# Value products of two attention heads issued in turn, one in each half of TensorE's columns

## The chip, the cores and the metric

One core of a Trainium2 chip runs the whole program. The metric is device time in microseconds of one execution; lower is better. The engines that matter here are TensorE (PE, with its weight loads listed as PEld), VectorE (DVE), ScalarE (ACT) and GpSimd (POOL).

## The reference

Two transformer-like blocks at 512 tokens and width 1024. What touches the change is its attention, always with heads of 64 values:

```python
# block 1: eight heads of dilated causal attention (beside a gated delta rule)
# block 2, even layer: eight neighbourhood heads, each of 512 queries over
#   a window of 256 keys and 256 context keys; eight heads of context over context;
#   and four differential heads of 128 values:
p1 = softmax(q1 @ k1.T * scale)
p2 = softmax(q2 @ k2.T * scale)
y  = (p1 - lam * p2) @ v
# block 2, odd layer: eight query heads over two key/value heads, 768 keys
p  = softmax(qg @ k.T * d ** -0.5)
y  = p @ v                      # the value product
```

## The kernel before

All attention works on tiles of 128 queries by 128 keys, in float32. For one head and one query tile there are four steps. *score*: TensorE writes the scores to PSUM, VectorE takes the row maximum, ScalarE the exponential into a tile E (helper `exp_rows`). *turn*: TensorE transposes E, 128 columns at a time, and ScalarE or VectorE copies the result into a tile PT (`pt_tiles`). *apply*: TensorE multiplies values and PT, one matmul for each key tile, summed in a PSUM bank `pv`. *end*: the bank is scaled by the row sums, which TensorE spreads over partitions with eight small matmuls on a tile `rr` (`bcast`, line 431), again 64 columns at a time.

Heads come in pairs. Head 0 of a pair has its result in partitions 0 to 63 of the bank, head 1 in 64 to 127. A value tile is 128 rows by 64 columns, so one product uses 64 of the array's 128 columns: head 0 the first half, head 1 the second. Before the change each head has an apply of its own, which runs through all its key tiles:

```python
for kt in range(qt + 1):
    c = (2 * pair + e) * 64
    PE.matmul(st["v", pair][hs, qs], self.dv[:, kt, c:c + 64], pt[:, kt * P:(kt + 1) * P],
              start=kt == 0, stop=kt == qt)
```

There are three such places: `dilated` (block 1, line 955, key tiles 1 to 4 by the query tile), `neighbourhood` (line 1664, 4 key tiles) and `pair_attention` (line 1723, the context heads of the even layer with 2 key tiles and the odd layer with 6). Differential attention (`diff_attention`, line 1779) uses all 128 columns and keeps its own apply; each of its query tiles makes two E tiles, e1 and e2, which VectorE (line 1764) and GpSimd (lines 1768 and 1769) merge into e1 before the transposes.

`skewing` sets the program order: in each round it calls, for items that follow one another, the later steps first. On top of it a scheduler with a timeline of its own orders the instructions of each engine when the program is built. At run time every engine takes its instructions in that order and waits on semaphores.

E, PT and q tiles come from rings of a fixed number of buffers; the writer of a new tile waits until the last reader of the tile that had that buffer is done. Before, E has 5 buffers in the even and odd layers, PT has 2.

Of the kernel before, what the change touches and what calls it, by code (L numbers as in the profile page):

```python
# [10 lines left out]
F32 = mybir.dt.float32  # L11
# [7 lines left out]
P = 128  # L19
D = 1024  # L20
KD = 8
T = 512
C = 256
TC = T + C
# [198 lines left out]
class Prog:  # L223
# [686 lines left out]
    def dilated(self, da, ps, om):  # L910
        V, S, G, PE, Q, A = self.V, self.S, self.G, self.PE, self.Q, self.A
        psa = lambda: self.bank(ps, "a")
        kzs = self.zeroed(da, T)
        st = {}
        items = []
        for pair in range(4):
            for qt in range(4):
                for e in range(2):
                    n = (qt + 1) * P
                    qs = slice(qt * P, (qt + 1) * P)  # L920
                    hs = slice(64 * e, 64 * e + 64)

                    def load(pair=pair, qt=qt, e=e, qs=qs):
                        if qt == 0:
                            strip = st["b", e] = da.tile([P, T], F32, name="strip", bufs=2)
                            Q.dma_start(strip, self.dstrip[2 * pair + e])
                            if e == 0:
                                room = self.wr.tile([P, CH], F32, name="wraw").bitcast(F32R)
                                st["k", pair] = self.stacked(da, self.dk[:, pair], "k", kz=kzs[pair % 2],
                                                             st=[room[:, :T], room[:, T:]])  # L930
                        if e == 0:
                            st["q", pair, qt] = self.doubled(da, self.dq[:, pair, qs], "q", 3)

                    def score(pair=pair, qt=qt, e=e, n=n, qs=qs, hs=hs):
                        if qt == 0 and e == 0:
                            st["r", pair] = da.tile([P, 4, 2], F32, name="rr", bufs=2)
                        p = psa()
                        (q, lo), (k, kz) = st["q", pair, qt], st["k", pair]
                        self.scores(p[:, :n], (q[:, e], lo), (k[e][:, :n], kz[e][:, :n]))
                        st["e", pair, qt, e] = self.exp_rows(da, p[:, :n], n, st["b", e][:, T - n:],  # L940
                                                             r=st["r", pair][:, qt, e:e + 1])[0]

                    def turn(pair=pair, qt=qt, e=e, n=n):
                        p = psa()
                        self.transpose4(p, st["e", pair, qt, e], qt + 1)
                        pt = st["t", pair, qt, e] = da.tile([P, T], F32, name="PT", tag="PT", bufs=2)
                        S.activation(pt[:, :n], p[:, :n], AF.Copy)

                    def apply(pair=pair, qt=qt, e=e, qs=qs, hs=hs):
                        if qt == 0 and e == 0:  # L950
# [12 lines left out]
        return items  # L963

    def finish_pair(self, pool, prb, pv, rr, dst, nt=4):

        n = nt * P
        for t in range(nt):
            for e in range(2):
                self.bcast(prb[64 * e:64 * e + 64, t * P:(t + 1) * P], rr[:, t, e:e + 1], 64)  # L970
        rs = pool.tile([P, T], F32, name="rs", tag="PT", bufs=2)
        self.S.activation(rs[:, :n], prb[:, :n], AF.Copy)
# [612 lines left out]
    def scores(self, p, q, k):  # L1585
# [22 lines left out]
    def neighbourhood(self, consts, values, at, ps, qa, ka, vc, vad, oms):  # L1608
# [5 lines left out]
        st = {}  # L1614
        items = []
        count = 0
        for pair in range(4):
            for b in range(4):
                x = (0, 1, 1, 2)[b]
                for e in range(2):  # L1620
# [22 lines left out]
                    def score(pair=pair, b=b, e=e, bt=bt):  # L1643
# [8 lines left out]
                        self.scores(p[:, 256:512], q, [a[:, T:TC] for a in k])  # L1652
                        st["e", pair, b, e] = self.exp_rows(at, p[:, 0:T], T, bt, TC, st["r", pair][:, b, e:e + 1], 5)[0]
# [4 lines left out]
                    def apply(pair=pair, b=b, e=e):  # L1658
                        if b == 0 and e == 0:
                            st["v", pair] = self.bank(ps, "pv")  # L1660
                        c = slice((2 * pair + e) * 64, (2 * pair + e) * 64 + 64)
                        for kt in range(4):
                            lhs = st["vw", b // 2][:, b % 2, kt, c] if kt < 2 else vc[:, kt - 2, c]
                            PE.matmul(st["v", pair][64 * e:64 * e + 64, b * P:(b + 1) * P], lhs,
                                      st["t", pair, b, e][:, kt * P:(kt + 1) * P], start=kt == 0, stop=kt == 3)

# [23 lines left out]
    def pair_attention(self, at, ps, qT, form, keys, nk, nq, vals, dst):  # L1690
# [6 lines left out]
        for t in range(nq):  # L1697
            for e in range(2):
                hs = slice(64 * e, 64 * e + 64)

                def load(t=t):
# [5 lines left out]
                def score(t=t, e=e):  # L1707
# [5 lines left out]
                    self.scores(p, q, st["k", e])  # L1713
                    st["e", t, e] = self.exp_rows(at, p[:, 0:n], n, None, TC, st["r"][:, t, e:e + 1], 5)[0]

                def turn(t=t, e=e):
                    st["t", t, e] = self.pt_tiles(at, ps, st["e", t, e], nk)

                def apply(t=t, e=e, hs=hs):
                    if t == 0 and e == 0:  # L1720
                        st["v"] = self.bank(ps, "pv")
                    for kt in range(nk):
                        PE.matmul(st["v"][hs, t * P:(t + 1) * P], vals(e, kt), st["t", t, e][:, kt * P:(kt + 1) * P],  # L1723
                                  start=kt == 0, stop=kt == nk - 1)
# [5 lines left out]
                items.append([load if e == 0 else None, None, score, turn, apply,  # L1730
                              end if t == nq - 1 and e == 1 else None])
        return items

    def diff_attention(self, at, ps, qkb, vb, lam, oms, kzs):
# [5 lines left out]
        for hd in range(4):  # L1740
            for t in range(6):
# [9 lines left out]
                def score(hd=hd, t=t, k0=k0, n=n):  # L1751
# [326 lines left out]
```

## Time and profile before

| what | value |
|---|---|
| median of 3 runs | 2650.19 us (2647.8 to 2650.38) |
| profiled execution, its own time | 2653.09 us |
| span of that execution, first to last instruction | 2651.1 us |
| TensorE busy | 94% of the span |
| VectorE, GpSimd, ScalarE busy | 62%, 45%, 38% |
| mean granted clock of TensorE | 0.973 of 2.4 GHz |

The profiled execution is 2.9 us above the median; 2.0 us of its time lie outside the span. The attention of the program lies in four stretches of the span: dilated (228 to 366 us), differential (1131 to 1250), neighbourhood and context (1250 to 1337), and the odd layer's (2084 to 2187.5).

### The profile page before, as it was taken

To read this page: it belongs to the slowest core of one execution; us is meant where nothing else is said; L and a number is where in the kernel's file an instruction comes from. 1 tells how busy PE (TensorE), PEld (TensorE's weight loads), DVE (VectorE), ACT (ScalarE), POOL (GpSimd) and SP (SyncE) were. 2 spreads that over 40 slices of the span, in tenths; PEclk is the share of its full clock that TensorE was granted. 3 is DMA by queue.
4 is the path that set the end of the run, shared out by engine and by line. 5 is a ranking of instruction groups with operands and counts; after the bars stand their busy time and mean duration, and the time that the engine had idled before them with its cause. 6 is when DMAs were issued, how large, how long until landed. Compare 5 with 4: busy or idle time off the path is not lost.

```text
span 2651.1 us, 35356 instructions
## 1 busy us (share of the span) xinstructions
PE 2500.5 (94%) x13312; PEld 2078.7 (78%) x13312; DVE 1631.5 (62%) x2896; ACT 996.5 (38%) x1763; POOL 1192.6 (45%) x835
## 2 busy tenths in 40 slices
PE   7878999999999987977999999999999999999999
PEld 5657876788888766766888888888888888788887
DVE  6987556635334798778747677767577446634333
ACT  4424534322224423377634222121244553323232
POOL 3346535555555443577623233323245326444443
PEclk9999999999999998988999999999999999999999
DMA  5252022232333344301132343424242104232333
GB/s 196 77 183 62 25 63 96 87 96 86 103 99 96 128 143 131 131 17 29 45 119 88 106 137 114 140 96 152 72 128 80 32 26 142 88 96 88 103 96 95
DMA packets 103453, 257.94 MB, mean 97 GB/s; under 512 B 11745, under 2 KB 20065, under 8 KB 102900
## 3 DMA queue, kind: packets, MB, share of 16 engines
q1 hardware_dynamic: 102708, 254.64, 29.8%
q8 instruction: 105, 1.72, 0.3%
q10 hardware_dynamic: 576, 1.05, 0.1%
q14 instruction: 64, 0.52, 0.1%
HBM read 246.06 MB, written 14.83 MB: 98 GB/s over the span
## 4 chain that ended last, share of the span: by engine, by line
PE 73%; DVE 17%; DMA 3%; issue 2%; POOL 2%; ACT 2%; SPq 0%; POOLq 0%; DVEq 0%; ACTq 0%
PE ps_mm L323 14%; PE ps_mm L325 14%; PE ps_mm L324 14%; PE ps_mx L324 3%; PE ps_mx L325 3%; PE ps_mx L323 3%; PE ps_m L324 3%; PE ps_m L323 3%; PE ps_m L325 3%; PE ps_t L435 2%; DVE ada_w L1094 2%; DVE ada_j L1094 2%; PE ps_s L1593 2%; PE ps_pv L1723 2%; DMA ada_w<-in_w_ada 2%
## 5 line engine op out<-in xcount | busy, mean ns | idle before, releaser
L312 POOL TENSOR_TENSOR wlo<-wraw,whi 128x1024 fp32r<-128x1024 f32 (+2 forms) x344 | 777.0, 2262 | 1102.1 <-ACT whi L311 1016.7
L311 ACT ACTIVATE whi<-wraw 128x1024 fp32r<-128x1024 f32 (+2 forms) x345 | 336.7, 978 | 955.0 <-PE ps_mm L324 473.2
L323 PE MATMUL ps_mm<-h,whi 128*128 128x512 f32 (+1 forms) x1496 | 540.5, 363 | 11.7 <-ACT whi L311 7.2
L325 PE MATMUL ps_mm<-h,wlo 128*128 128x512 f32 (+1 forms) x1496 | 539.3, 361 | 2.6 <-POOL wlo L312 2.5
L324 PE MATMUL ps_mm<-h,whi 128*128 128x512 f32 (+1 forms) x1496 | 539.5, 361 | 1.1 <-DVE h L1146 1.0
L323 PEld LDWEIGHTS ps_mm<-h,whi 128*128 128x128 f32 x1496 | 282.1, 189 | 56.8 <-ACT whi L311 7.2
L325 PEld LDWEIGHTS ps_mm<-h,wlo 128*128 128x128 f32 x1496 | 281.9, 189 | 49.1 <-POOL wlo L312 3.2
L324 PEld LDWEIGHTS ps_mm<-h,whi 128*128 128x128 f32 x1496 | 282.1, 189 | 47.6 <-issue 1.7
L1094 DVE CUSTOM_DVE_ANT_0 ada_j<-ada_w,ada_c 128x512 f32<-128x512 f32 x192 | 184.3, 960 | 13.1 <-DMA ada_w<-in_w_ada 12.6
L325 PE MATMUL ps_mm<-fa,wlo 128*128 128x512 f32 (+1 forms) x528 | 186.2, 356 | 1.7 <-POOL wlo L312 1.7
L1094 DVE CUSTOM_DVE_ANT_0 ada_w<-ada_w,ada_c 128x512 f32<-128x512 f32 x192 | 185.2, 965 | 4.0
L324 PE MATMUL ps_mm<-fa,whi 128*128 128x512 f32 (+1 forms) x528 | 187.6, 356 | 0.0
L323 PE MATMUL ps_mm<-fa,whi 128*128 128x512 f32 (+1 forms) x528 | 185.8, 356 | 0.0
L1271 DVE SCALAR_TENSOR_TENSOR cb<-ps_mm,small,cb 128x511 f32<-128x511 f32 (+1 forms) x66 | 43.6, 660 | 188.8 <-ACT cb L1269 188.8
L1219 DVE SCALAR_TENSOR_TENSOR x<-ps_mm,mod,x 128x512 f32<-128x512 f32 x80 | 59.5, 748 | 138.5 <-PE ps_mm L325 131.7
L325 PEld LDWEIGHTS ps_mm<-fa,wlo 128*128 128x128 f32 x528 | 99.0, 188 | 18.2 <-POOL wlo L312 2.3
L323 PEld LDWEIGHTS ps_mm<-fa,whi 128*128 128x128 f32 x528 | 98.9, 188 | 16.6 <-ACT whi L311 0.5
L324 PEld LDWEIGHTS ps_mm<-fa,whi 128*128 128x128 f32 x528 | 99.2, 188 | 16.0
L435 PE MATMUL ps_t<-ident,E 128*128 128x128 f32 x464 | 79.9, 292 | 20.4 <-POOL E L1769 13.6
L903 DVE TENSOR_REDUCE nm<-ps_s 128x1 f32<-128x768 f32 (+1 forms) x96 | 73.7, 774 | 38.7 <-PE ps_s L1593 37.8
L324 PE MATMUL ps_mx<-h,whi 128*128 128x512 f32 x216 | 86.2, 399 | 3.0 <-DVE h L1006 3.0
L323 PE MATMUL ps_mx<-h,whi 128*128 128x512 f32 x216 | 85.7, 398 | 0.5 <-ACT whi L311 0.5
(500 smaller groups left out, 5239.1 us busy)
## 6 DMA issues: line engine op xcount, KB each, us to landing
ada_w<-in_w_ada SPq DMA_DIRECT2D x192, 256.0 KB
wraw<-in_w_up SPq DMA_DIRECT2D x88, 512.0 KB
wraw<-in_w_d SPq DMA_DIRECT2D x48, 384.0 KB
wraw<-in_w_d SPq DMA_DIRECT2D x53, 320.0 KB
wraw<-in_we_in SPq DMA_DIRECT2D x24, 512.0 KB
wraw<-in_w_g SPq DMA_DIRECT2D x22, 512.0 KB
wraw<-in_w_u SPq DMA_DIRECT2D x22, 512.0 KB
wraw<-in_we_out SPq DMA_DIRECT2D x13, 512.0 KB
```

The source lines that it names most:

```text
L311: self.S.activation(hi[:, :n], raw[:, :n], AF.Copy)
L312: (eng or self.G).tensor_tensor(out=lo[:, :n], in0=raw[:, :n], in1=hi.bitcast(F32)[:, :n], op=ALU.subtract)
L323: mm(ps, lhi, rhi, start=start, stop=False)
L324: mm(ps, lhi, rlo, start=False, stop=False)
L325: mm(ps, llo, rhi, start=False, stop=stop)
L435: last = self.PE.transpose(ps[:, j * P:(j + 1) * P], src[:, j * P:(j + 1) * P], self.ident)
L903: V.tensor_reduce(out=m, in_=src, op=ALU.max, axis=AX.X, negate=True)
L1094: V.tensor_tensor_reduce(out=(junk, w)[s], in0=w, in1=c[:, s, i * T:i * T + T], scale=0.5, scalar=0.0, op0=ALU.mult, op1=ALU.add, accum_ou ...
L1219: V.scalar_tensor_tensor(out=xs[s][:, m], in0=p[:, :w], scalar=mod[:, gate * 8 + m, s:s + 1], in1=xs[s][:, m], op0=ALU.mult, op1=ALU.add)
L1271: V.scalar_tensor_tensor(out=cb[:, t0 + 1:t1], in0=pg[s][:, :w_ - 1], scalar=fw[0], in1=cb[:, t0 + 1:t1], op0=ALU.mult, op1=ALU.add)
L1593: self.PE.matmul(p[:, c0:min(n, c0 + 512)], q[i], k[i][:, c], start=i == 0, stop=i == 1)
L1723: PE.matmul(st["v"][hs, t * P:(t + 1) * P], vals(e, kt), st["t", t, e][:, kt * P:(kt + 1) * P], start=kt == 0, stop=kt == nk - 1)
```

## The change

A new helper issues the products of both heads of a pair in one step, key tile by key tile, head 0 and head 1 in turn. It runs in the item of head 1, when both PT tiles exist. To hold two PT tiles longer, PT goes from 2 to 3 buffers everywhere; E goes from 5 to 4 in the even and odd layers, and q from 3 to 2 in the dilated one.

```diff
@@ dilated
-                            st["q", pair, qt] = self.doubled(da, self.dq[:, pair, qs], "q", 3)
+                            st["q", pair, qt] = self.doubled(da, self.dq[:, pair, qs], "q", 2)
...
-                        pt = st["t", pair, qt, e] = da.tile([P, T], F32, name="PT", tag="PT", bufs=2)
+                        pt = st["t", pair, qt, e] = da.tile([P, T], F32, name="PT", tag="PT", bufs=3)
...
-                        pt = st["t", pair, qt, e]
-                        for kt in range(qt + 1):
-                            c = (2 * pair + e) * 64
-                            PE.matmul(st["v", pair][hs, qs], self.dv[:, kt, c:c + 64], pt[:, kt * P:(kt + 1) * P],
-                                      start=kt == 0, stop=kt == qt)
+                        self.apply_pair(st["v", pair], qs, qt + 1,
+                                        lambda e, kt: self.dv[:, kt, (2 * pair + e) * 64:(2 * pair + e) * 64 + 64],
+                                        [st["t", pair, qt, e] for e in range(2)])
...
-                    items.append([load if qt == 0 or e == 0 else None, None, score, turn, apply,
+                    items.append([load if qt == 0 or e == 0 else None, None, score, turn, apply if e else None,
@@ new helper, and pt_tiles
+    def apply_pair(self, pv, cols, nk, vals, pts):
+        for kt in range(nk):
+            for e in range(2):
+                self.PE.matmul(pv[64 * e:64 * e + 64, cols], vals(e, kt), pts[e][:, kt * P:(kt + 1) * P],
+                               start=kt == 0, stop=kt == nk - 1)
...
-        pt = at.tile([P, 6 * P], F32, name="PT")
+        pt = at.tile([P, 6 * P], F32, name="PT", bufs=3)
@@ neighbourhood and pair_attention call it in the same way
-                    items.append([load, None, score, turn, apply, end if b == 3 and e == 1 else None])
+                    items.append([load, None, score, turn, apply if e else None, end if b == 3 and e == 1 else None])
@@ diff_attention (the same 5 to 4 in neighbourhood and pair_attention)
-                        es.append(self.exp_rows(at, p[:, :n], n, None, TC, bufs=5))
+                        es.append(self.exp_rows(at, p[:, :n], n, None, TC, bufs=4))
```

The scheduler places the products. In the odd layer's attention TensorE has, before the change, the products of one head (6, here also split as 4 and 2) between transposes (`ps_t<-ident,E`) and scores (`ps_s`); `gv` are the values:

```order
L1723 MATMUL ps_pv<-PT,gv 64x128 x6
L435 MATMUL ps_t<-ident,E 128x128 x4
L1593 MATMUL ps_s<-kh,qs 128x512
L1593 MATMUL ps_s<-kl,qs 128x512
L1593 MATMUL ps_s<-kh,qs 128x256
L1593 MATMUL ps_s<-kl,qs 128x256
L1723 MATMUL ps_pv<-PT,gv 64x128 x4
L435 MATMUL ps_t<-ident,E 128x128 x2
L1723 MATMUL ps_pv<-PT,gv 64x128 x2
L435 MATMUL ps_t<-ident,E 128x128 x4
```

The same place of TensorE's order with the change; the products now stand at line 1596:

```order
L435 MATMUL ps_t<-ident,E 128x128 x4
L1589 MATMUL ps_s<-kh,qs 128x512
L1589 MATMUL ps_s<-kl,qs 128x512
L1589 MATMUL ps_s<-kh,qs 128x256
L1589 MATMUL ps_s<-kl,qs 128x256
L435 MATMUL ps_t<-ident,E 128x128 x2
L1596 MATMUL ps_pv<-PT,gv 64x128 x12
```

The twelve products of a pair now stand together in one row of the order, head 0 and head 1 in turn, where each head had its own.

In the neighbourhood, TensorE's order before (`vw` and `vctx` are window and context values):

```order
L435 MATMUL ps_t<-ident,E 128x128 x12
L1664 MATMUL ps_pv<-PT,vw_10004 64x128 x2
L1664 MATMUL ps_pv<-PT,vctx 64x128 x2
L1664 MATMUL ps_pv<-PT,vw_10004 64x128 x2
L1664 MATMUL ps_pv<-PT,vctx 64x128 x2
L1593 MATMUL ps_s<-whi,qd 128x256
```

And with the change:

```order
L435 MATMUL ps_t<-ident,E 128x128 x4
L1596 MATMUL ps_pv<-PT,vw_10004 64x128 x4
L1596 MATMUL ps_pv<-PT,vctx 64x128 x4
L435 MATMUL ps_t<-ident,E 128x128 x4
L1596 MATMUL ps_pv<-PT,vw_10004 64x128
L1589 MATMUL ps_s<-wlo,qd 128x256
```

Here the two heads' products stood next to each other before already, head after head (2 and 2, then 2 and 2); now they alternate, and the first product of the next pair is sent ahead alone, with the other seven of that pair a few rows later.

## Rows read from the trace of the kernel before

**Rows 1.** The page: busy time, share of the span and count of each engine.
```profile
PE 2500.5 (94%) x13312; PEld 2078.7 (78%) x13312; DVE 1631.5 (62%) x2896; ACT 996.5 (38%) x1763; POOL 1192.6 (45%) x835
```

**Rows 2.** Busy time by stretch: length, engines with counts, granted clock, DMA.
```profile
228.00:366.00 138.00, 133.75 (x1142) 113.67 (x1142) 79.86 (x214) 74.74 (x177) 79.39 (x110) 0.98 0.08 25
1131.00:1250.00 119.00, 92.05 (x557) 80.39 (x557) 93.60 (x224) 92.76 (x251) 93.11 (x125) 0.87 0.08 22
1250.00:1337.00 87.00, 80.10 (x698) 68.86 (x696) 61.37 (x171) 55.41 (x148) 50.63 (x80) 0.96 0.15 47
2084.00:2187.50 103.50, 103.47 (x778) 85.81 (x779) 51.06 (x104) 57.46 (x116) 18.80 (x29) 1.00 0.06 17
```

**Rows 3.** Groups in 2084 to 2187.5: shapes, count, busy us, mean ns, idle before.
```profile
L1723 PE MATMUL ps_pv<-PT,gv 128*64 128x128 f32 x384 | 49.7, 279 | 0.1
L1723 PEld LDWEIGHTS ps_pv<-PT,gv 128*64 128x64 f32 x384 | 39.2, 136 | 7.1 <-issue 3.5 <-ACT PT L1603 0.8 <-DVE PT L1605 0.3
...
L904 ACT ACTIVATE E<-ps_s,nm 128x768 f32<-128x768 f32 x31 | 27.8, 898 | 8.7 <-DVE nm L903 8.3 <-DVE rr L907 0.3
```

**Rows 4.** Timeline of TensorE: start us, us, line, operation, count; three places.
```profile
2088.31 1.52 PE L1723 MATMUL ps_pv<-PT,gv 128*64 128x128 f32 x12
2089.76 0.50 PE L323 MATMUL ps_t<-h,whi 128*128 128x512 f32 x1
...
2123.70 1.09 PE L1723 MATMUL ps_pv<-PT,gv 128*64 128x128 f32 x8
2124.72 0.76 PE L435 MATMUL ps_t<-ident,E 128*128 128x128 f32 x5
...
2178.49 0.44 PE L435 MATMUL ps_t<-ident,E 128*128 128x128 f32 x2
2178.86 0.65 PE L1723 MATMUL ps_pv<-PT,gv 128*64 128x128 f32 x4
2179.45 0.66 PE L435 MATMUL ps_t<-ident,E 128*128 128x128 f32 x4
```

**Rows 5.** Timeline of TensorE: matmuls of both halves close together.
```profile
1270.41 1.09 PE L431 MATMUL ps_t<-ident,rr 128*64 128x128 f32 x15
...
1274.86 0.67 PE L1723 MATMUL ps_pv<-PT,vctx 128*64 128x128 f32 x8
1275.45 0.39 PE L1593 MATMUL ps_s<-whi,qd 128*128 128x256 f32 x1
```

**Rows 6.** Products by stretch (length, TensorE busy and count): neighbourhood, then dilated.
```profile
1250.00:1337.50 87.50, 39.10 (x320) 30.56 (x320) 4.12 (x8) 0.00 (x0) 0.96 0.16 49
228.00:366.00 138.00, 24.18 (x160) 16.66 (x160) 0.98 0.08 25
```

**Rows 7.** Who TensorE waited for in 1131 to 1250: total us, times, longest.
```profile
PE ps_t L435 <- POOL E L1769: 13.6, 13, 1.9
```

**Rows 8.** Timeline in 1131 to 1250: exponentials, and transposes of two tiles earlier.
```profile
1139.01 0.88 ACT L904 ACTIVATE E<-ps_s,nm 128x768 f32<-128x768 f32 x1
1139.67 0.44 PE L435 MATMUL ps_t<-ident,E 128*128 128x128 f32 x2 [0.52 <-POOL E L1769]
...
1203.14 0.47 ACT L904 ACTIVATE E<-ps_s,nm 128x256 f32<-128x256 f32 x1
1203.41 0.44 PE L435 MATMUL ps_t<-ident,E 128*128 128x128 f32 x2 [1.86 <-POOL E L1769]
1207.12 0.47 ACT L904 ACTIVATE E<-ps_s,nm 128x256 f32<-128x256 f32 x1
...
1237.51 0.46 ACT L904 ACTIVATE E<-ps_s,nm 128x256 f32<-128x256 f32 x1
1238.56 0.69 PE L435 MATMUL ps_t<-ident,E 128*128 128x128 f32 x2 [1.91 <-POOL E L1769]
```

**Rows 9.** Groups in 1130 to 1250, columns as in rows 3.
```profile
L1768 POOL TENSOR_SCALAR E<-E,er 128x256 f32<-128x256 f32 x16 | 23.0, 1440 | 13.8 <-DVE er L1762 9.3 <-ACT E L904 3.2 <-DVE rsq_a L300 1.2
...
L1769 POOL TENSOR_TENSOR E<-E 128x256 f32<-128x256 f32 x16 | 13.7, 857 | 0.5
```

More of the change, by code (lines that the diff above doesn't have):

```diff
@@ L920, in dilated @@
                     qs = slice(qt * P, (qt + 1) * P)
-                    hs = slice(64 * e, 64 * e + 64)
                     def load(pair=pair, qt=qt, e=e, qs=qs):
@@ L931, in load, with score @@
                         if e == 0:
-                            st["q", pair, qt] = self.doubled(da, self.dq[:, pair, qs], "q", 3)
-                    def score(pair=pair, qt=qt, e=e, n=n, qs=qs, hs=hs):
+                            st["q", pair, qt] = self.doubled(da, self.dq[:, pair, qs], "q", 2)
+                    def score(pair=pair, qt=qt, e=e, n=n, qs=qs):
                         if qt == 0 and e == 0:
@@ L945, in turn, with apply @@
                         self.transpose4(p, st["e", pair, qt, e], qt + 1)
-                        pt = st["t", pair, qt, e] = da.tile([P, T], F32, name="PT", tag="PT", bufs=2)
+                        pt = st["t", pair, qt, e] = da.tile([P, T], F32, name="PT", tag="PT", bufs=3)
                         S.activation(pt[:, :n], p[:, :n], AF.Copy)
-                    def apply(pair=pair, qt=qt, e=e, qs=qs, hs=hs):
-                        if qt == 0 and e == 0:
+                    def apply(pair=pair, qt=qt, qs=qs):
+                        if qt == 0:
                             st["v", pair] = self.bank(ps, "pv")
-                        pt = st["t", pair, qt, e]
-                        for kt in range(qt + 1):
-                            c = (2 * pair + e) * 64
-                            PE.matmul(st["v", pair][hs, qs], self.dv[:, kt, c:c + 64], pt[:, kt * P:(kt + 1) * P],
-                                      start=kt == 0, stop=kt == qt)
+                        self.apply_pair(st["v", pair], qs, qt + 1,
+                                        lambda e, kt: self.dv[:, kt, (2 * pair + e) * 64:(2 * pair + e) * 64 + 64],
+                                        [st["t", pair, qt, e] for e in range(2)])
                     def end(pair=pair):
                         self.finish_pair(da, psa(), st["v", pair], st["r", pair], om[:, :, 4 + pair, :])
-                    items.append([load if qt == 0 or e == 0 else None, None, score, turn, apply,
+                    items.append([load if qt == 0 or e == 0 else None, None, score, turn, apply if e else None,
                                   end if qt == 3 and e == 1 else None])
@@ L970, in finish_pair @@
                 self.bcast(prb[64 * e:64 * e + 64, t * P:(t + 1) * P], rr[:, t, e:e + 1], 64)
-        rs = pool.tile([P, T], F32, name="rs", tag="PT", bufs=2)
+        rs = pool.tile([P, T], F32, name="rs", tag="PT", bufs=3)
         self.S.activation(rs[:, :n], prb[:, :n], AF.Copy)
@@ L1652, in score, with apply, vals @@
                         self.scores(p[:, 256:512], q, [a[:, T:TC] for a in k])
-                        st["e", pair, b, e] = self.exp_rows(at, p[:, 0:T], T, bt, TC, st["r", pair][:, b, e:e + 1], 5)[0]
+                        st["e", pair, b, e] = self.exp_rows(at, p[:, 0:T], T, bt, TC, st["r", pair][:, b, e:e + 1], 4)[0]
                     def turn(pair=pair, b=b, e=e):
                         st["t", pair, b, e] = self.pt_tiles(at, ps, st["e", pair, b, e], 4)
-                    def apply(pair=pair, b=b, e=e):
-                        if b == 0 and e == 0:
+                    def apply(pair=pair, b=b):
+                        if b == 0:
                             st["v", pair] = self.bank(ps, "pv")
[L1661 to L1665, printed above, removed]
+                        def vals(e, kt):
+                            c = slice((2 * pair + e) * 64, (2 * pair + e) * 64 + 64)
+                            return st["vw", b // 2][:, b % 2, kt, c] if kt < 2 else vc[:, kt - 2, c]
+                        self.apply_pair(st["v", pair], slice(b * P, (b + 1) * P), 4, vals,
+                                        [st["t", pair, b, e] for e in range(2)])
                     def end(pair=pair):
@@ L1698, in pair_attention @@
             for e in range(2):
-                hs = slice(64 * e, 64 * e + 64)
                 def load(t=t):
@@ L1713, in score, with apply @@
                     self.scores(p, q, st["k", e])
-                    st["e", t, e] = self.exp_rows(at, p[:, 0:n], n, None, TC, st["r"][:, t, e:e + 1], 5)[0]
+                    st["e", t, e] = self.exp_rows(at, p[:, 0:n], n, None, TC, st["r"][:, t, e:e + 1], 4)[0]
                 def turn(t=t, e=e):
                     st["t", t, e] = self.pt_tiles(at, ps, st["e", t, e], nk)
-                def apply(t=t, e=e, hs=hs):
-                    if t == 0 and e == 0:
+                def apply(t=t):
+                    if t == 0:
                         st["v"] = self.bank(ps, "pv")
-                    for kt in range(nk):
-                        PE.matmul(st["v"][hs, t * P:(t + 1) * P], vals(e, kt), st["t", t, e][:, kt * P:(kt + 1) * P],
-                                  start=kt == 0, stop=kt == nk - 1)
+                    self.apply_pair(st["v"], slice(t * P, (t + 1) * P), nk, vals, [st["t", t, e] for e in range(2)])
                 def end():
@@ L1728, in end @@
                     self.finish(at, ps, st["v"], st["r"], (to[:, 0], to[:, 1]), nq)
-                items.append([load if e == 0 else None, None, score, turn, apply,
+                items.append([load if e == 0 else None, None, score, turn, apply if e else None,
                               end if t == nq - 1 and e == 1 else None])
```

## The prediction

> **What bounds the kernel now.** The page comes first: TensorE is busy 94% of the span [rows 1]. That is an average, so the table by stretch comes next, for the four stretches with attention [rows 2]. In the odd layer's attention TensorE is busy 103.47 of 103.50 us at full clock, VectorE and ScalarE near half. In the dilated stretch it is busy 133.75 of 138, in the neighbourhood 80.10 of 87. So a microsecond of TensorE time that goes away in these three should mostly leave the run. Differential attention is another case: TensorE 92 of 119 us, the other three engines 93 to 94 each, and TensorE waits 13.6 us in it for GpSimd's last merge of E [rows 7]. No engine is full there; the stretch is a chain that passes through all four, and it has no products that the change touches, only the ring of E that it shortens.
>
> In the timeline of TensorE [rows 4, 5] look at start times, not at durations, since matmuls overlap. One float32 product is two records in the trace: 384 for the odd layer's 192 [rows 3].
>
> **What alternation is worth for one run.** Twelve records of one head start at 2088.31 and the next instruction at 2089.76: 1.45 us. Eight take 1.02 (2123.70 to 2124.72), four 0.59 (2178.86 to 2179.45) [rows 4]. That is 0.145 us for the run and 0.109 for each record. Two rows show both halves. Eight records that are two products of head 0 and two of head 1 take 0.59 (1274.86 to 1275.45), as long as four of one head. The spreading matmuls on rr have the same shape as the products and alternate halves already: fifteen records in 1.09 us, so (1.09 - 0.27) / 14 = 0.059 between starts, 0.27 being the duration of one [rows 5]. So the halves run side by side, and a run costs 0.145 + 0.109 x (records of its busier half). A run also has an entry: from the second transpose (2178.49 + 0.44 - 0.27 = 2178.66) to the first product is 0.20 us, where one transpose follows another after about 0.11 [rows 4]; a run more or less is thus worth 0.145 + 0.09 = 0.24 us.
>
> The Trainium skill has a rule that speaks against this. "TensorE: Matmul & The Clock Gate", Part 3 (The mechanism), says a weight load overlaps matmuls in flight only when it goes to another row group; the two halves use all 128 rows, so by it each load would wait and alternation bring nothing, although a table on the same page lists column tiles as concurrent. By that rule the gains below would all be zero. A load here takes 136 ns on average [rows 3], and alternating records start 59 ns apart [rows 5], so the trace already contradicts it, and I take the rows.
>
> **The change, part by part.** I counted runs and busier halves in TensorE's order, before and with the change.
>
> *Odd layer.* 16 pair tiles of 6 products for each head. A pair that goes in one run saves 12 records x 0.109 = 1.31 us and a run; one whose first product goes ahead alone saves 10 x 0.109 = 1.09 us, with as many runs. Nine of the 16 are of that kind. Over the whole stretch, spreading matmuls included: 43 runs with 398 serial records become 36 with 248. Before: 43 x 0.145 + 398 x 0.109 = 49.6 us; rows 3 has 49.7 busy for the products. After: 36 x 0.145 + 248 x 0.109 = 32.3. Gain 17.3 + 7 x 0.09 = 18 us. With TensorE the only full engine, and ScalarE's 57.5 us against the 85 that remain, I let 17 through.
>
> *Neighbourhood and context.* 39.1 us of products [rows 6], but the heads often stood next to each other, and then their runs overlap in part already. 32 runs with 318 serial records become 39 with 240: 39.3 us to 31.8, less 7 entries at 0.09: 7 us. The first third of the stretch is not full on TensorE, so I let 6 through. The bounds are 0 and 12, if all 416 records there (spreading included) were halved to 208.
>
> *Dilated.* Key tiles n = 1 to 4. With the first product ahead, a pair tile saves (n - 1) x 2 x 0.109: 0, 0.22, 0.44, 0.65, together 1.31 for each of four pairs: 5.2 us of the 24.2 [rows 6]. If all alternated, half the 160 records, 8.7 us. TensorE is full to 97%, but the gated delta rule beside it is a chain of its own: I take 4, bounds 0 and 8.7.
>
> *Waiting for the second head.* All products of a pair now need head 1's PT. A late PT would stop TensorE and all that is queued behind: transposes and scores of the next tiles, and with them VectorE's maxima. In the order, transposes and scores of other tiles stand between head 1's last transposes and the run, so the copy has some 1 to 2 us to land. Zero; what it could cost is the first rival. The third PT buffer removes waits of the copying engines, which are not full: zero. The q ring of 2 in the dilated part: GpSimd is busy 79 of 138 us there, zero.
>
> *E from 5 to 4 buffers.* This can cost. In differential attention tile t uses two E. With 5, the first exponential of tile t reuses the second E of tile t - 3, long merged. With 4 it reuses e1 of tile t - 2, and must wait until TensorE has transposed that. I compared each exponential of the stretch with those transposes. Of 44, twelve now start earlier than they then may: from the first (exponential at 1139.01, transposes done at 1139.67 + 0.44 = 1140.11) to the last (1237.51 against 1238.56 + 0.69), 12.9 us in sum, 1.1 us each [rows 8]. The bounds are 0 and 12.9. Most are short tiles with room behind them: at 1203.14 the wait would be 0.7 us, and ScalarE's next exponential is at 1207.12 [rows 8]. The loop itself is short: transposes 0.7, two exponentials of 0.9 [rows 3], GpSimd 1.44 and 0.86 [rows 9], some 5 us, and it turns once in two tiles, which now take 2 x 119 / 24 = 9.9. I take 3. In the neighbourhood and the odd layer the transposes that free a buffer stand well ahead of the scores that need it in nearly all places: zero.
>
> **Sum.** -17 - 6 - 4 + 3 = -24 us. Against the profiled execution: 2653.1 - 24 = 2629.1. It lies 2.9 above the median, so 2626 us.
>
> **The rivals.**
> - *Part is given back to new waits* in the odd layer and the neighbourhood, where two copies of PT, maxima and exponentials must now keep up with a faster TensorE. For: ScalarE already waits 8.3 us for VectorE's maxima in the odd layer [rows 3]. Against: about half of both engines' time there is idle [rows 2]. Half of the 23 lost: 2626 + 11.5 = 2638.
> - *The ring of four costs its full 12.9.* For: the stretch is a chain, and its clock of 0.87 says that TensorE's pauses there already cost speed. Against: the room at 1203. 2626 + 10 = 2636.
> - *Slower: the ring of four takes over differential attention.* Each of its 24 tiles would be held up, since a late exponential also holds a score bank. From 32 us, 1.35 a tile, it outweighs the 27 of gains and 0.2% more, the least that a measurement of this kernel tells from no change; at 1.5 a tile 2650 - 27 + 36 = 2659. Against: the loop of 5 us in a period of 9.9.
> - *It doesn't do what it says*: the halves don't overlap, as the page's rule has it. Then only the 3 us remain: 2653. Rows 5 speak against it.
>
> **How the numbers follow.** Forecast 0.60, waits 0.14, full ring 0.14, slower by the ring 0.04, no overlap 0.04; 0.04 for a gain below the range. The most that the terms allow is 18 + 12 + 8.7 at no cost, 2611; I cut the range at 2614. The first two rivals end near 2637, and a mixture of them a few us higher. Range 2614 to 2641. Faster by over 0.2% (under 2644.9): the first three and the larger gain, less a little for mixtures: 0.88. Same 0.07, slower 0.05.
>
> **What would show it.** Right: odd attention some 86 us long, still full on TensorE; product records 55 to 60 ns apart inside runs; the products' busy time near 32 us there; neighbourhood some 6 us shorter, dilated 4. Wrong: spacing of 109 ns in alternating runs; TensorE idle before products for PT; ScalarE's exponentials in differential attention waiting for transposes, and that stretch over 125 us.

## The result, and the profile after

The changed kernel takes 2614.37 us (median of 4 runs, 2606.63 to 2619.97), the kernel before, beside it, 2648.99 us (4 runs, 2645.15 to 2650.38): a ratio of 0.987 with an interval of 0.9841 to 0.9898. In a second set of runs the same kernel stood at 0.9887 (0.9867 to 0.9907) of the kernel before. So the gain is 30 to 35 us, where 24 were forecast. The profiled execution of the changed kernel took 2619.97 us with a span of 2618.2, against 2653.09 and 2651.1 before: 33 us less.

The page's row of TensorE, which answers to [rows 1]:

```profile
PE 2474.6 (95%) x13312; PEld 2051.2 (78%) x13312; DVE 1631.3 (62%) x2896; ACT 993.6 (38%) x1763; POOL 1194.1 (46%) x835
```

The number of matmul records is the same; TensorE is busy 25.9 us less. The same four stretches as in [rows 2], from their first score or product to their last product (length, busy time of TensorE, its loads, VectorE, ScalarE and GpSimd with counts, granted clock, DMA share and GB/s):

```profile
224.90:364.30 139.40, 129.24 (x1147) 109.28 (x1145) 83.93 (x226) 76.49 (x180) 81.81 (x112) 0.96 0.08 25
1126.00:1241.00 115.00, 88.17 (x543) 76.53 (x542) 95.64 (x217) 88.76 (x245) 89.50 (x120) 0.90 0.08 22
1243.00:1323.00 80.00, 74.17 (x701) 60.39 (x699) 59.08 (x171) 55.73 (x150) 52.04 (x82) 0.96 0.15 44
2068.90:2153.40 84.50, 84.05 (x775) 68.73 (x775) 49.54 (x102) 57.23 (x114) 18.40 (x29) 1.00 0.06 20
```

The last line is the one to look at first: the odd layer's attention has 775 matmul records in 84.50 us, and TensorE is still full. The kernel before, between the same instructions, has as many in 102.60:

```profile
2084.00:2186.60 102.60, 102.57 (x775) 85.04 (x775) 50.37 (x103) 57.43 (x115) 18.80 (x29) 1.00 0.05 16
```

The groups of that stretch, which answer to [rows 3], and the products alone in the neighbourhood and in the dilated stretch, which answer to [rows 6]:

```profile
L1596 PE MATMUL ps_pv<-PT,gv 128*64 128x128 f32 x384 | 30.7, 280 | 0.4 <-ACT PT L1607 0.4
...
L904 ACT ACTIVATE E<-ps_s,nm 128x768 f32<-128x768 f32 x31 | 27.9, 900 | 4.3 <-DVE nm L903 3.5
L1596 PEld LDWEIGHTS ps_pv<-PT,gv 128*64 128x64 f32 x384 | 22.8, 136 | 5.5 <-issue 3.0 <-ACT PT L1607 1.0 <-ACT E L904 0.2
```

```profile
1243.00:1323.00 80.00, 29.62 (x320) 20.53 (x320) 0.96 0.15 44
224.90:364.30 139.40, 17.66 (x160) 10.87 (x160) 0.96 0.08 25
```

One record of a product lasts as long as before (280 ns on average, 279 in [rows 3]), but the busy time of all 384 has gone from 49.7 to 30.7 us, in the neighbourhood from 39.1 to 29.6 and in the dilated stretch from 24.2 to 17.7. In the odd layer TensorE waited 0.4 us, once, for a PT. In the timeline of TensorE (start, duration, line, operation, count) the runs themselves:

```profile
2084.25 0.44 PE L435 MATMUL ps_t<-ident,E 128*128 128x128 f32 x2
2084.61 0.43 PE L1596 MATMUL ps_pv<-PT,gv 128*64 128x128 f32 x2
2084.98 0.88 PE L435 MATMUL ps_t<-ident,E 128*128 128x128 f32 x6
...
2087.84 1.53 PE L1596 MATMUL ps_pv<-PT,gv 128*64 128x128 f32 x24
2089.31 0.87 PE L435 MATMUL ps_t<-ident,E 128*128 128x128 f32 x6
2091.95 1.52 PE L1596 MATMUL ps_pv<-PT,gv 128*64 128x128 f32 x22
2093.40 0.44 PE L435 MATMUL ps_t<-ident,E 128*128 128x128 f32 x2
```

Read the starts: 24 records, a whole pair, take 2089.31 - 2087.84 = 1.47 us, as long as the twelve of one head did before [rows 4]. Where a pair's run has 22 records, its first product has gone ahead alone, as at 2084.61, where it takes 0.37 us by itself.

### The profile page after: what moved, and what is told of

Same layout as the page of the kernel before. It is cut to its first block, busy times and chain, and to the rows that moved or that the text cites. A ratio compares the mean times of both kernels' runs of the same rounds, so it can differ in the third digit from the quotient of the medians.

```text
span 2618.2 us, 35313 instructions
## 1 busy us (share of the span) xinstructions
PE 2474.6 (95%) x13312; PEld 2051.2 (78%) x13312; DVE 1631.3 (62%) x2896; ACT 993.6 (38%) x1763; POOL 1194.1 (46%) x835
## 4 chain that ended last, share of the span: by engine, by line
PE 72%; DVE 16%; DMA 3%; ACT 3%; issue 3%; POOL 3%; SPq 0%; POOLq 0%; DVEq 0%; ACTq 0%
PE ps_mm L323 14%; PE ps_mm L325 14%; PE ps_mm L324 14%; PE ps_mx L324 3%; PE ps_mx L325 3%; PE ps_mx L323 3%; PE ps_m L324 3%; PE ps_m L323 3%; PE ps_m L325 3%; PE ps_pv L1596 2%; DVE ada_j L1090 2%; PE ps_s L1589 2%; DVE ada_w L1090 2%; PE ps_t L435 2%; DMA ada_w<-in_w_ada 2%
## 5 line engine op out<-in xcount | busy, mean ns | idle before, releaser
L1090 DVE CUSTOM_DVE_ANT_0 ada_j<-ada_w,ada_c 128x512 f32<-128x512 f32 x192 | 189.7, 988 | 13.7 <-DMA ada_w<-in_w_ada 13.3
L1090 DVE CUSTOM_DVE_ANT_0 ada_w<-ada_w,ada_c 128x512 f32<-128x512 f32 x192 | 179.9, 937 | 4.0
L903 DVE TENSOR_REDUCE nm<-ps_s 128x1 f32<-128x768 f32 (+1 forms) x96 | 74.1, 774 | 28.4 <-PE ps_s L1589 27.1
L324 PE MATMUL ps_mx<-h,whi 128*128 128x512 f32 x216 | 86.3, 399 | 3.2 <-DVE h L1002 3.2
```

The lines of the kernel that those rows point to most:

```text
L324: mm(ps, lhi, rlo, start=False, stop=False)
L903: V.tensor_reduce(out=m, in_=src, op=ALU.max, axis=AX.X, negate=True)
L1090: V.tensor_tensor_reduce(out=(junk, w)[s], in0=w, in1=c[:, s, i * T:i * T + T], scale=0.5, scalar=0.0, op0=ALU.mult, op1=ALU.add, accum_ou ...
```

## The experiments

Lengths of stretches below are taken from the trace of each kernel's profiled execution, from the first score (differential attention) or the first product (the other two) to the end of the last product; the last column is TensorE's busy time for the odd layer's products.

| kernel | median, us | ratio to before | differential | neighbourhood | odd layer | its products |
|---|---|---|---|---|---|---|
| before | | | 118.9 | 86.3 | 102.7 | 49.7 |
| changed | 2614.37 | 0.987 (0.9841 to 0.9898) | 115.4 | 79.9 | 84.5 | 30.7 |
| changed, again | 2621.36 | 0.9887 (0.9867 to 0.9907) | 115.4 | 80.8 | 84.5 | 30.7 |
| rings only | 2646.18 | 0.9985 (0.9974 to 0.9996) | 117.5 | 90.5 | 96.6 | 44.2 |
| head after head in the joint step | 2645.54 | 0.9986 (0.9972 to 1.0) | 118.0 | 89.7 | 96.8 | 44.5 |
| turns on the old rings | 2624.11 | 0.9891 (0.9871 to 0.9911) | 117.1 | 79.4 | 86.0 | 32.2 |
| head 1 first | 2611.61 | 0.986 (0.9842 to 0.9879) | 117.3 | 78.0 | 76.6 | 26.2 |
| head 1 first, again | 2614.28 | 0.9868 (0.9849 to 0.9887) | 116.8 | 77.0 | 76.1 | 26.2 |
| all of head 1, then all of head 0 | 2632.42 | 0.9936 (0.9918 to 0.9954) | 116.5 | 81.8 | 89.5 | 40.6 |
| turns of two products | 2616.08 | 0.9865 (0.9844 to 0.9887) | 116.9 | 78.6 | 77.2 | 27.1 |
| before, ring of four E | 2651.81 | 0.9995 (0.9982 to 1.0008) | 115.5 | 86.1 | 102.7 | 49.7 |
| before, ring of three E | 2657.93 | 1.0019 (1.001 to 1.0028) | 121.1 | 88.6 | 103.0 | 50.0 |
| head 1 first, old rings | 2610.52 | 0.9852 (0.9827 to 0.9876) | 119.0 | 76.5 | 76.4 | 26.4 |

The odd layer's column starts at the first product, and that hides something: from the first score to the first product pass 8.4 to 8.9 us in the kernels that begin with head 0 and 12.8 in those that begin with head 1. From the first score on, the odd layer takes 111.1 us before, 93.3 with the change and 89.3 with head 1 first.

The kernel before ran beside each set, with medians of 2649.95 us (the first four experiments), 2651.26 (the next four) and 2652.61 (the last three).

**The rings alone.** The kernel before, with the three sizes of the change and nothing else:

```diff
-  pt = ... name="PT", tag="PT", bufs=2)
+  pt = ... name="PT", tag="PT", bufs=3)
-  self.exp_rows(..., bufs=5)        # E, three places
+  self.exp_rows(..., bufs=4)
-  self.doubled(da, self.dq[:, pair, qs], "q", 3)
+  self.doubled(da, self.dq[:, pair, qs], "q", 2)
```

> The products stay head after head, each head in a step of its own, as before; only the rings are those of the change (PT 3, E 4, q 2). Theory: the gain comes from the halves taking turns, and the rings alone bring almost nothing. Counted in TensorE's order, all half-array runs together cost 147.4 us before and 145.3 here (0.235 us a run and 0.109 for each record of its busier half), so -2, and in the odd layer alone -6 with +4 in the neighbourhood. The ring of four E costs 3 us in differential attention by the forecast: 2649 - 2 + 3 = 2650, a ratio of 1.000. Rival, the rings: the third PT buffer lets the copies run ahead, and it is what made differential attention 3.5 us shorter and part of the odd layer's 18: 2649 - 3.5 - 6 = 2640 or below, and the differential stretch 116 us long instead of 119.

Measured: 0.9985, between the 2650 of the theory and the 2640 of the rival; the odd layer 6.0 us shorter, the neighbourhood 4.2 longer, as counted. With other rings the scheduler puts other instructions side by side. Some 4 us (1 to 7 by the interval) of the 30 to 35 can be theirs.

**Joint step, head after head.** The changed kernel with the two loops of `apply_pair` exchanged:

```diff
-  for kt in range(nk):
-      for e in range(2):
+  for e in range(2):
+      for kt in range(nk):
```

> As the changed kernel in everything, rings and joint step too, but in the joint step head 0's products all go before head 1's. Theory, taking turns is what counts: the half-array runs cost 145.1 us by the same count, against 124.0 with turns and 147.4 before, so the time is 2649 - 2, with the 3.5 of differential attention if the rings brought it 2643, else 2647; the odd layer's attention some 97 us long (-6). Rival, standing together is enough: the two heads' runs, end to end, overlap where they meet, or TensorE takes a half's loads ahead over many records; then 2614 to 2620, the odd layer's attention 85 us.

Measured: 0.9986, the gain is gone. But this kernel doesn't separate the two theories as meant: head 0's PT is ready first, and the scheduler lets its products go ahead, so that in TensorE's order the heads stand apart nearly as in the run with the rings alone (133 half-array runs, 134 there, 141 before). A better test follows below, with all of head 1 first.

**Turns on the old rings.** The changed kernel with PT 2, E 5 and q 3 again:

> As the changed kernel, products in turn, but on the rings of before (PT 2, E 5, q 3). Theory: the half-array runs cost 123.1 us (124.0 in the changed kernel), so the gain stays. If the ring of four E costs its 3 us in differential attention, this is 3 us quicker than the changed kernel, 2611; if rings of the change are what shortened that stretch by 3.5, 2618, and its stretch is 119 us again. In the odd layer 38 runs instead of 33 make 89 us instead of 85 (+4), in the neighbourhood -1.4. Rival, the third PT buffer is needed because the joint step holds two PT until head 1's is ready: TensorE then waits for PT copies before transposes, half of the gain goes, 2632 or more, and the transposes show waits for ScalarE and VectorE.

Measured: 2624, above either number, yet its ratio of 0.9891 can't be told from the changed kernel's 0.987 and 0.9887. The odd layer takes 86.0 us, where 89 were counted, and the neighbourhood 79.4; TensorE's only wait in the odd layer is 0.9 us for an exponential, none is for a PT. The rings aren't needed for the gain; the rival's 2632 lies above all six runs (2611.19 to 2626.36).

**Head 1 first.** In the changed kernel head 0's first product often goes ahead by itself, since its PT is there first. Here each turn begins with head 1:

```diff
   for kt in range(nk):
-      for e in range(2):
+      for e in (1, 0):
```

> As the changed kernel, but each turn begins with head 1, whose PT is ready last, so that no product of head 0 goes ahead by itself. TensorE's order has 31 such lone first products in the changed kernel (11 in dilated attention, 11 in the neighbourhood, 9 in the odd layer) and none here. Theory, entries and serial records cost what the count says: 140 half-array runs with 836 serial records (124.0 us) become 107 with 754 (107.3 us), -17 us of TensorE's time; in the odd layer -5 of 85, in the neighbourhood -6 of 80 at most, the rest in dilated attention, of which less comes through. I expect -12 against the changed kernel: 2602. Rival: a lone product filled a gap in which TensorE would wait for head 1's PT; then those waits come back as idle time before products, the busy time falls and the span doesn't: 2614, ratio to the changed kernel 1.000.

> Head 1 first in each turn once more, beside the changed kernel on one chip. Theory: 8 us shorter in the odd layer's attention as in e4_second (77 us against 85), 2 in the neighbourhood, 1 to 3 in dilated attention, some 4 of it lost again where the odd layer starts, because no lone product fills the time to head 1's PT: 6 us quicker than the changed kernel, a ratio of 0.9977. Rival: the first profile only happened to be quick; ratio 1.000 within 0.001.

Measured: 2611.61 and 2614.28, where 2602 was expected at first. From its first product on, the odd layer's attention is 8 us shorter both times (76.6 and 76.1 us), with its products at 26.2 us. But half of the 8 has only moved: nothing is sent ahead, so that scores and transposes which stood behind the first product now stand in front of it (12.8 us instead of 8.8). From the first score on, the odd layer is 4.0 us shorter in the first set and 4.6 in the second; 5 were expected. In the second set, where both ran on one chip, the ratios are 0.9868 and 0.9887 with intervals that overlap, so that a gain of some 5 us over the changed kernel is likely but not established.

**All of head 1, then all of head 0.** As the run before, with the loops exchanged. No product of head 0 can go ahead. In the odd layer eight of the 16 pairs then stand in one run without turns; in the other eight the scheduler sends four products of head 1 ahead:

```diff
-  for kt in range(nk):
-      for e in (1, 0):
+  for e in (1, 0):
+      for kt in range(nk):
```

> Against the run with head 1 first in each turn (e4_second, 2612): the same joint step, which waits for head 1's PT, but all of head 1's products and then all of head 0's, in one unbroken run. This is joint issue without turns. Theory, halves overlap only where products of the two heads are neighbours, with a look-ahead of some four records: a run of 6 and 6 products takes 0.145 + 24 x 0.109 less about 0.38, 2.4 us, instead of 1.45; in the odd layer 16 x 0.93 = +15 us (its attention 92 us instead of 77), in neighbourhood and context +6, in dilated attention +2: 2612 + 22 = 2634. Rival, what counts is that both heads stand in one run: 2612 again, and twelve and twelve records in 1.45 us.

**Turns of two products.** The same, with two key tiles of head 1, two of head 0, and so on:

```diff
+  for k0 in range(0, nk, 2):
+      for e in (1, 0):
+          for kt in range(k0, min(nk, k0 + 2)):
```

> Against the run with head 1 first in each turn (e4_second, 2612): the turns are two products (four records) of a head instead of one. Theory, with a look-ahead of some four records a half's stretch of four costs nothing: 2612, ratio to e4_second 1.000, the odd layer's attention 77 us. Rival, only direct neighbours overlap: a run of 6 and 6 products has five changes of half, each hides one record, so 19 serial records instead of 12: 0.76 us a run, +12 in the odd layer, +6 in the neighbourhood: 2630.

Measured: 2632.42 for the blocks (2634 expected) and 2616.08 for the turns of two (2612). The three timelines of TensorE show the same 24 records with the instruction behind them: first the turns of one (head 1 first), then the blocks, then the turns of two.

```profile
2084.82 1.53 PE L1596 MATMUL ps_pv<-PT,gv 128*64 128x128 f32 x24
2086.28 0.88 PE L435 MATMUL ps_t<-ident,E 128*128 128x128 f32 x6
```

```profile
2095.52 2.45 PE L1596 MATMUL ps_pv<-PT,gv 128*64 128x128 f32 x24
2097.91 0.88 PE L435 MATMUL ps_t<-ident,E 128*128 128x128 f32 x6
```

```profile
2087.78 1.58 PE L1597 MATMUL ps_pv<-PT,gv 128*64 128x128 f32 x24
2089.29 0.88 PE L435 MATMUL ps_t<-ident,E 128*128 128x128 f32 x6
```

1.46, 2.39 and 1.51 us. (The kernel before has runs of 24 records too, head after head, and the one at 2117.39 also takes 2.39.) Without any overlap it would be 0.145 + 24 x 0.109 = 2.76, by the price of a run. So a run of two blocks hides 0.37 us, three to four records, and no more; standing together is not enough. Stretches of four records of one half cost almost nothing, 0.05 us.

This settles what the joint step with head 0 first left open, though not wholly for the turns. From the start of each run to the next instruction, spreading matmuls included, the odd layer's half-array runs take 49.9 us before, 42.5 in blocks and 28.5 in turns, head 1 first. So two thirds of the saving there need the turns; one third comes with the joint step, which makes 24 runs out of 43 and lets the heads meet. In the whole kernel the blocks gain 17 us and the turns 35.

**The changed kernel again**, beside the last three:

> The changed kernel once more, unaltered, so that it stands on the same chip beside the next one: 2614 to 2618, differential attention 115 to 118 us (the spread that this stretch showed over executions in which nothing in it differs but the ring of E).

Measured: 2621.36, 0.9887: 4 us less gain than in the first set, which is how far two measurements of the same ratio lie apart here.

**The ring of E by itself.** The kernel before with `bufs=5` of E set to 4, and to 3:

> The kernel before with one edit: the ring of E has 4 buffers, not 5 (PT 2, q 3, products head after head). Forecast's step: +3 us in differential attention, 119 to 122 us. Theory now: the exponentials do wait for E (some 4 us more of ScalarE's idle time before them in this stretch), but ScalarE waited nearly as long before its PT copies, and that wait shrinks by as much; the stretch stays at 117 to 119 us and the whole at 2650, ratio 1.000. Rival: four buffers do cost 3 us and the third PT buffer, which came with them, gives them back; then 122 us here and a ratio of 1.001.

> The kernel before with 3 buffers of E. Now an exponential must wait for the tile one earlier: the second exponential of a tile can't start before the first E of the tile ahead is transposed, and that comes after two merges on GpSimd (1.44 and 0.86 us). If buffers of E can bound the differential stretch at all, it shows here: a round of two exponentials, reciprocals, merges and transposes of some 5 us in nearly each of 24 tiles becomes the period, 24 x 5 = 120 or more, so 119 becomes 125 to 145 us. Rival: the stretch is bound by something else and has room even at three: 119 us. The neighbourhood and the odd layer use the same three and may lose too; what is read is the differential stretch.

Measured: with four, 0.9995 (0.9982 to 1.0008, or 5 us quicker to 2 slower), and 115.5 us in differential attention, 3.4 less than in the one profile of before and below the 117 to 119 expected. With three, 1.0019 and 121.1 us, under the 125 expected. Both kernels have the products of before, head after head. What the ring of four does is seen in ScalarE's groups of that stretch (busy us, mean ns, idle time before them and who ended it), before and then with four:

```profile
L904 ACT ACTIVATE E<-ps_s,nm 128x768 f32<-128x768 f32 (+1 forms) x48 | 36.1, 753 | 3.8 <-DVE nm L903 3.0 <-DVE er L907 0.4
L1603 ACT ACTIVATE PT<-ps_t 128x512 f32<-128x512 f32 (+1 forms) x24 | 12.5, 521 | 6.6 <-PE ps_t L435 6.6
...
L1579 ACT ACTIVATE qd<-qkb 128x256 fp32r<-128x256 f32 x21 | 8.7, 415 | 6.1 <-PE ps_s L1593 6.0
```

```profile
L904 ACT ACTIVATE E<-ps_s,nm 128x768 f32<-128x768 f32 (+1 forms) x48 | 36.3, 757 | 7.7 <-DVE nm L903 4.0 <-POOL E L1769 1.4 <-DVE er L1762 1.2
L1603 ACT ACTIVATE PT<-ps_t 128x512 f32<-128x512 f32 (+1 forms) x24 | 12.5, 519 | 3.6 <-PE ps_t L435 3.6
...
L1579 ACT ACTIVATE qd<-qkb 128x256 fp32r<-128x256 f32 x21 | 8.7, 417 | 3.6 <-PE ps_s L1593 3.6
```

The exponentials do wait longer, 7.7 us instead of 3.8, and the merges on GpSimd now stand among the releasers. But the copies of PT wait 3.0 us less and those of q 2.5. The wait has moved within ScalarE; it hasn't been added: ScalarE idles 26.3 us of the stretch in both profiles.

**Head 1 first, old rings.** PT 2, E 5, q 3, and the turns that begin with head 1:

> Head 1 first in each turn, on the rings of before (PT 2, E 5, q 3). Half-array runs 107.1 us by the count, as with head 1 first on the changed rings (107.3). Theory: the rings hardly matter, 2612 to 2617. Rival: since the joint step holds two PT and none of its products goes ahead, the transposes of the next tile find no free PT of the two: TensorE waits for both products before it can go on with transposes, 2625 or more, with waits of TensorE for copies of PT in the odd layer.

Measured: 2610.52, 0.9852 (0.9827 to 0.9876), with 76.4 us in the odd layer and no wait of TensorE in it for a PT. The rival falls. This is the quickest kernel of the study by its median, and it needs none of the three rings; its interval overlaps that of head 1 first on the changed rings and that of the changed kernel.

## Why the prediction was right, and where it was off

The sign and the main mechanism held. The first median, 2614.37 us, lies 0.4 us inside the low end of the range, one of its four runs (2606.63) below it, and the second, 2621.36, well inside; that the first fell inside is in part luck. Two terms were wrong, the ring of E and the dilated attention; that their errors cancel in the sum is luck as well. By stretch, in the profiled executions (the first set, then the kernel run again):

| term | forecast | changed | again |
|---|---|---|---|
| odd layer | -17 | -18.1 | -18.1 |
| neighbourhood and context | -6 | -6.3 | -5.4 |
| dilated | -4 | -4.0 | -2.5 |
| differential attention | +3 | -3.5 | -3.6 |
| all else | 0 | -1.1 | -9.3 |
| sum | -24 | -33.0 | -38.9 |

- **The price of a run** held. The forecast's 0.145 + 0.109 x (records of the busier half) gives 1.45 us for 24 records in turn, and the trace has 1.46 to 1.47. Its sums for the odd layer, 49.6 and 32.3 us, include the spreading matmuls; counted in the same way, from the start of each run to the next instruction, the traces have 49.9 in 43 runs and 32.9 in 36. The forecast set its 49.6 beside the 49.7 of [rows 3], which are busy time of the products alone; that these agree is chance.
- **Odd layer, neighbourhood**: both as counted. TensorE stayed full in the odd layer, and the rival that half would be given back to new waits fell: TensorE waited 0.4 us for a PT there, and ScalarE's exponentials wait less than before for maxima (3.5 us instead of the 8.3 in [rows 3]).
- **Dilated**: the -4 was too much; at most some 1 us is the change's. The stretch holds one wait from before its first product: after the first score TensorE waits for ScalarE's copies of the values (`dv`, line 890), 7.6 us before, and then 4.8 and 5.5 (changed, again):

```profile
PE ps_p L435 <- ACT dv L890: 7.6, 1, 7.6
PE ps_p L435 <- ACT dv L890: 4.8, 1, 4.8
PE ps_p L435 <- ACT dv L890: 5.5, 1, 5.5
```

It differs between executions of one kernel: with head 1 first it is 4.7 us in one profile and 7.6 in the other, and the stretches of 138.0 and 141.3 us differ by it. Without this wait the stretch takes 135.7 us before, 134.5 and 135.3 with the change, 133.3 and 133.7 with head 1 first. Rings alone, head after head and the ring of four are 0.7 to 1.4 shorter than before as well, turns on the old rings not at all. So TensorE's 6.5 us less for products (from [rows 6] to 17.7), or 12.0 with head 1 first, bring 0 to 1 and some 2 us. TensorE isn't full there, and its other waits in the stretch grew from 3.3 to 5.2 us, 2.9 of them a single new one before the spreading matmuls. That the gated delta rule beside it sets the rest was argued and not tested.
- **The ring of E is the step that failed.** The forecast said: "With 4 it reuses e1 of tile t - 2, and must wait until TensorE has transposed that", 12.9 us late in sum, of which 3 were taken. In the program the buffers aren't handed out by turns but in the order in which they come free: with four, e1 of a tile takes the place of e2 of tile t - 2, which the merge frees, and e2 takes that of e1. The trace of the changed kernel shows it at a place where it matters; columns as in the timelines above:

```profile
1143.54 0.73 POOL L1771 TENSOR_TENSOR E<-E 128x256 f32<-128x256 f32 x1
...
1144.30 0.47 ACT L904 ACTIVATE E<-ps_s,nm 128x256 f32<-128x256 f32 x1 [1.25 <-DVE er L1764]
...
1144.34 0.42 PE L435 MATMUL ps_t<-ident,E 128*128 128x128 f32 x2
```

The merge ends at 1144.27, the exponential starts at 1144.30, and the transposes that it was supposed to wait for start with it, at 1144.34. (The row names VectorE's `er`, which ends at 1144.28 as well; the semaphore on which the exponential's record waits is GpSimd's, so it is the merge.) In all, ten first exponentials of the stretch start before the transposes of tile t - 2 have ended, in the changed kernel as in the kernel before with a ring of four; that e1 always follows the merge is inferred from this. Counted again in the trace of before with the buffers as they are really handed out, the lateness is 6.1 us over eleven exponentials, not 12.9 over twelve. And of that ScalarE's other waits give back nearly all, as in the run with four buffers. The rest of the stretch goes on as before: TensorE's wait for the last merge, 13.6 us in [rows 7], is now

```profile
PE ps_t L435 <- POOL E L1771: 13.4, 12, 2.5
```

With four buffers the stretch took 115.4 to 118.0 us in nine profiles, with five 118.9, 117.1 and 119.0, so that it is, if anything, some 2 us shorter; its granted clock was 0.87, 0.90 and 0.87 in these three and 0.90 to 0.93 in the nine. Whether the clock or the order makes this difference stays open; the ratio of 0.9995 says that it is worth nothing that these runs can tell over the whole kernel. The step should have been 0.
- **What remains.** With 18 in place of 17, 1 in place of 4 and 0 in place of +3 the sum is -25. The measured 30 to 35 leave 5 to 10. Of these, differential attention has 3.5 in both profiles, with its cause open, and two measurements of the same ratio already differ by 4. The -9.3 of "all else" in the second profile is mostly not the change's. From 375 to 415 us, behind the dilated part, the rows of before, changed and changed again are (columns as above, the clock is third from the end):

```profile
375.00:415.00 40.00, 36.35 (x171) 25.70 (x170) 15.69 (x49) 6.95 (x15) 8.10 (x9) 0.83 0.41 127
375.00:415.00 40.00, 37.89 (x169) 27.32 (x169) 14.12 (x45) 7.75 (x16) 8.77 (x9) 0.79 0.37 115
375.00:415.00 40.00, 37.87 (x204) 28.72 (x202) 15.88 (x57) 9.45 (x17) 14.15 (x11) 1.00 0.44 140
```

The two profiles of the changed kernel have TensorE busy equally long, but in the one with the clock granted in full 204 of its records start there, in the other 169. That execution, with 2613.98 us, was the quickest of its six (median 2621.36). So single profiles of one kernel can lie some 8 us apart in a place that the change doesn't touch.
- **The rival from the skill** fell. In the runs above 24 loads of 136 ns on average [rows 3] and their matmuls fit into 1.46 us, 61 ns for each, though both halves use all rows of the array; within one half, too, the records follow each other after 109 ns, less than a load. The Trainium skill ("TensorE: Matmul & The Clock Gate", Part 3, The mechanism) has a load overlap matmuls in flight only when it goes to another row group; by that rule the odd layer would have stayed at 102 us, and the measurement decides against it for halves of the columns.

## What to carry to other kernels

Two matmuls that each use half of the array's columns ran side by side here if they were neighbours in TensorE's order. The price of a run is then that of its busier half, and it paid in full where TensorE was full (18 us in the odd layer) and hardly where it was not (at most some 1 us in the dilated part). Turns of one or two float32 products of a head did it, blocks of six did not; nothing between them was run. In a joint step let the operand that is ready last come first, or single products leak out ahead of the turns and pay an entry of their own; that was worth 4 us in the odd layer. When a ring of buffers is shortened, find out in which order its buffers really come back before naming what will have to wait, and look whether the engine that waits was waiting for something else anyway.

## What the runs showed of the hardware

- The records of the two halves start almost together and not evenly spaced: in the run of 22 records at 2072.59 us they start in pairs 6 to 7 ns apart, and the pairs follow each other after 109 ns, which is the spacing within one half. The page of the Trainium skill that was named above has tiles in different row groups start at most 4 ns apart ("TensorE: Matmul & The Clock Gate", Why this matters for your kernels), and in this the trace nearly agrees. The forecast had them "55 to 60 ns apart", which is only the mean.
- TensorE looks ahead over few records. In the run of two blocks (twelve records of each half) eight records start at 109 ns spacing, then eight in two interleaved rows of 109, then eight at 109 again: the second half starts with the ninth record of the first, when three more are still to come. Four records side by side, 4 x 0.109, less the 57 ns by which the two rows are shifted, are the 0.37 us. There the records don't name their half, and it is read from the spacing. In the neighbourhood of the kernel before they do: in TensorE's order each head has window values (`vw`) and then context values (`vctx`), and in the trace the second head's `vw` starts beside the first head's first `vctx`, with three of the latter to come:

```profile
1251.02 0.65 PE L1664 MATMUL ps_pv<-PT,vw 128*64 128x128 f32 x4
1251.50 0.27 PE L1664 MATMUL ps_pv<-PT,vctx 128*64 128x128 f32 x1
1251.51 0.32 PE L1664 MATMUL ps_pv<-PT,vw 128*64 128x128 f32 x1
1251.61 0.27 PE L1664 MATMUL ps_pv<-PT,vctx 128*64 128x128 f32 x1
```

- A product that goes alone between full-width matmuls costs 0.37 us (2084.61 to 2084.98). In its pair's run its two records would add next to nothing, since the other half is the busier one there: 22 records take 1.45 us (2091.95 to 2093.40) and 24 take 1.47. Without these lone products the odd layer's half-array runs went from 32.9 to 28.5 us, in 27 runs instead of 36; 5 us had been counted.
